# Forgetting attention in a two-layer decoder trunk: the running sums of log f enter the scores by an addition on VectorE instead of by matmuls

## The chip, the cores and the metric

The kernel runs on one core of one Trainium2 chip. The metric is the device time of one execution in microseconds. Before the change the median of three executions is 919.61 us (918.66 to 920.67).

## What is computed

A residual trunk of two layers works on 256 rows of width 2048. In each layer one normalised input is multiplied by one wide weight matrix, and the product feeds four groups of four heads: forgetting attention ("fox"), differential attention, block attention ("moba") and gated linear attention ("gla"). Their outputs are gated, joined and multiplied by an output matrix. The change touches only the fox group, of which this is the core:

```python
cum = jnp.cumsum(log_f.astype(jnp.float32), axis=-1)
logits = jnp.einsum("bhqd,bhkd->bhqk", q_i, k) * scale
logits = logits + c_i[..., :, None] - cum[:, :, None, :]
logits = jnp.where(k_pos[None, :] <= q_pos[:, None], logits, -jnp.inf)
p = jax.nn.softmax(logits, axis=-1)
```

Here `log_f` is the log-sigmoid of one number per row and head. The part that depends on the query alone falls out of the softmax, so the kernel adds only a row that runs over the keys, one row for each head.

## The kernel before

**The steps.** Each weight matrix is cut into blocks of up to 512 columns, and each block into steps of two or four tiles of 128 rows. For one step, SyncE issues the load of `raw` (L1106), ScalarE rounds it to `hi` (L426), VectorE subtracts to get `lo` (L429), and TensorE does 12 matmuls, or 24 for narrow blocks: the input's high part by `hi`, its low part by `hi`, its high part by `lo` (L1192 to L1196). `hi` and `lo` have four buffers each, so these two engines can prepare at most three steps beyond the one that TensorE is on. `raw` has four buffers as well. Blocks 0, 1 and 2 of a layer (gla's gate, gla's q and k, and a block that holds the four `fox_f` columns) run interleaved; block 2 accumulates in a `side` tile.

**The small work.** Everything else is written as generators in a list `tasks`. After each step's matmuls, `tick` (L257) goes through the list in order and lets each task emit instructions up to its next `yield`. It stops when the estimated cost put on VectorE or ScalarE passes what TensorE's work has allowed (L261, L1202). So the order of each engine's instructions is fixed when the program is built; an engine then executes its own list strictly in that order and waits for others by semaphores. A small product that is emitted after step n stands between step n and step n+1 in TensorE's list. Helpers `matmul` (L276) and the cost wrapper (L178) record most instructions, which is why the profile shows them under these two lines.

**The forgetting bias.** When block 2 is finished, `gla_gate` (L569) copies `fox_f` to `fx` and starts `fox_forget` (L812). This adds the bias, computes the log-sigmoid through three small ScalarE activations on `fe` (Abs, Exp, Ln; L529), forms `f` on VectorE and scales it. Then it rounds `f` to `fh` with a rest `fl`, and ScalarE multiplies two constant 128x128 triangles (`since`, part of the tile `ct`) by every column of both, 8 activations of 128x128 for each part and layer. The two results stay in two `four` tiles. Later `softmax_part` (L703) lets TensorE sum them over the partitions: a matmul with a tile of ones, `ones_r`, puts the row into all partitions of the score tile, and the head's product of q and k is accumulated on top. There are two such matmuls of 512 columns for each half of the keys, so six in a layer. VectorE adds the causal mask `neg4`, takes the maximum, and ScalarE does the exponentials.

**The gated linear attention beside it.** The task `gla` (L591) runs at the same time. It goes through ScalarE and VectorE to fill the tile `eight`, and issues groups of seven products `side<-tq,eight` (L661 to L664), which stand in TensorE's list between steps.

Of the kernel before, what the change touches and what calls it, by code (L numbers as in the profile page):

```python
# [13 lines left out]
F32 = mybir.dt.float32  # L14
F32R = mybir.dt.float32r
BF16 = mybir.dt.bfloat16
U8 = mybir.dt.uint8
AF = mybir.ActivationFunctionType
# [3 lines left out]
P = 128  # L22
# [185 lines left out]
def hybrid_trunk(  # L208
# [39 lines left out]
    def take_side():  # L248
        return (yield from side.take([P, 1024]))
# [24 lines left out]
    def matmul(out, lhsT, rhs, start, stop, tiles=1):  # L274
        left["pe"] += int(np.prod(rhs.shape[1:])) * (4 if lhsT.dtype == F32 else 1) / 2400.0 / tiles
        t_.matmul(out, lhsT, rhs, start=start, stop=stop)  # L276
# [70 lines left out]
    dng = cp.tile([P, DEPTH], F32, name="dng")  # L347
    gng = cp.tile([P, DEPTH], F32, name="gng")
    wa = cp.tile([17, DEPTH, 256], F32, name="wa")
    ones_r = cp.tile([P, P], F32R, name="ones_r")  # L350
    neg_b = cp.tile([P, P], BF16, name="neg_b")
    neg4 = neg_b[:, None, :].to_broadcast([P, H, P])
    halfpow = cp.tile([P, 8], F32, name="halfpow")
# [21 lines left out]
    def constants():  # L375

        yield from until(("h", 0, 3))
        nc.scalar.dma_start(wa[0:16], gla_wa2.rearrange("l r e -> r l e"))
        nc.scalar.dma_start(wa[16:17].rearrange("p l e -> p (l e)"), gla_ba.rearrange("(o l) e -> o (l e)", o=1))
        yield  # L380
        c, n = CAT["masks"]
        mb = s4.get([P, n], BF16)
        nc.scalar.dma_start(mb, const_b[:, c:c + n])
        yield
        c, n = CAT["neg"]
        nc.scalar.dma_start(neg_b, const_b[:, c:c + n])
        nc.scalar.dma_start(gng, gla_norm_gt)
        nc.scalar.dma_start(fb.rearrange("p l h -> p (l h)"), bcast_rows(fox_fb, 0, DEPTH * H))
        yield
        lamt = s2.get([P, DEPTH, 4, 64])  # L390
        nc.scalar.dma_start(lamt.rearrange("p l a d -> p (l a d)"), bcast_rows(diff_lam, 0, DEPTH * 256))
        nc.scalar.dma_start(dng, diff_norm_gt)
        yield
        v_.tensor_copy(masks.rearrange("p l t -> p (l t)"), mb)
        v_.tensor_scalar(ones_r, ident, 0.0, 1.0, op0=OP.mult, op1=OP.add)
        s4.put(mb)
        ready.add("constants")
        yield
        lp = s2.get([P, DEPTH, 2, 64])
        for l in range(DEPTH):  # L400
            v_.tensor_mul(lp[:, l], lamt[:, l, 0:4:2], lamt[:, l, 1:4:2])
            v_.tensor_reduce(ls2[:, l], lp[:, l], axis=AX.X, op=OP.add)
        s2.put(lp, lamt)
        yield
        a_.activation(ls2, ls2, AF.Exp)
        yield
        for l in range(DEPTH):
            li = 0.8 - 0.6 * math.exp(-0.3 * l)
            v_.scalar_tensor_tensor(lam[:, l:l + 1], ls2[:, l, 0:1], li, ls2[:, l, 1:2], op0=OP.add, op1=OP.subtract)
            v_.tensor_scalar(dng[:, l:l + 1], dng[:, l:l + 1], 1.0 - li, None, op0=OP.mult)  # L410
# [14 lines left out]
    def hi_of(hi, src, scale=1.0):  # L425
        a_.activation(hi, src, AF.Copy, scale=scale)  # L426

    def lo_of(lo, src, hi):
        v_.tensor_sub(lo, src, hi.bitcast(F32))  # L429
# [139 lines left out]
    def gla_gate(l, ps):  # L569
        r, sg = env["r", l], env["gla_sg", l]  # L570
        vn = s4.get([P, 2, GW])
        fx = sm.tile([P, 2, H], F32, name="fx", bufs=2)
        for m in range(2):
            a_.activation(fx[:, m], ps[m][:, 180:184], AF.Copy, scale=r[:, m:m + 1])
            a_.activation(sg[:, m, 332:], ps[m][:, :180], AF.Silu, scale=r[:, m:m + 1])
            a_.activation(vn[:, m, :164], ps[m][:, 184:], AF.Copy, scale=r[:, m:m + 1])
        env["fox_v", l] = vn
        env["forget", l] = Forget()
        tasks.append(fox_forget(l, fx, env["forget", l]))

    def gla_v(l, ps):

# [120 lines left out]
    def softmax_part(m, qT, kT, rows, scale, su, forget=None):  # L703

        ps = yield from take_side()
        S = ps.rearrange("p (j h s) -> p j h s", j=2, h=H)
        for kt in range(m + 1):
            dst = S[:, kt]
            if forget is not None:
                forget(dst, kt)  # L710
            for h in range(H):
                matmul(dst[:, h], qT[rows, m * H + h], kT[1][rows, kt * H + h],
                       forget is None, forget is None or h == H - 1)
        yield
        v_.tensor_add(S[:, m], S[:, m], neg4)
        mx = sm.tile([P, H], F32, name="mx")
        if m == 0:
            v_.tensor_reduce(mx, S[:, 0], axis=AX.X, op=OP.max)
        else:
            v_.tensor_reduce(mx, S.rearrange("p j h s -> p h j s"), axis=AX.XY, op=OP.max)  # L720
        nb = sm.tile([P, H], F32, name="nb")
        v_.tensor_scalar(nb, mx, -scale, None, op0=OP.mult)
        yield
        if m == 0:
            p = yield from s2.take([P, H, P])
        else:
            p = yield from s4.take([P, H, 2, P])
        for h in range(H):
            a_.activation(p[:, h], S[:, 0, h] if m == 0 else S[:, :, h], AF.Exp, bias=nb[:, h:h + 1], scale=scale,
                          accum_out=su[:, m, h:h + 1])  # L730
            if h == 1:
                yield
        side.put(ps)
        return p
# [7 lines left out]
    def attend(l, gi, name, qT, kT, forget=None):  # L742

        su = sm.tile([P, 2, H], F32, name="su")
        rs = sm.tile([P, 2, H], F32, name="rs")
        boxes = []
        for m, pool in enumerate((s2, s4)):
            p = yield from softmax_part(m, qT, kT, slice(0, P), HD ** -0.5, su, forget)
            if m:
                s4.put(qT, kT[0])  # L750
                if forget is not None:
                    forget.release()
            v_.reciprocal(rs[:, m], su[:, m])
            for h in range(H):
                a_.activation(p[:, h], p[:, h], AF.Copy, scale=rs[:, m, h:h + 1])
            yield
            boxes.append(spawn(turned_p(p, m, partial(pool.put, p))))
        yield from until((name + "_v", l))
        yield from until((name + "_g", l))
        t0, p0 = yield from joined(boxes[0])  # L760
        t1, p1 = yield from joined(boxes[1])
        yield
        vn, (sgt, sg) = env[name + "_v", l], env[name + "_g", l]
        ops = yield from take_side()
        o = ops.rearrange("p (m h t) -> p m h t", m=2, h=H)
        for h in range(H):
            v0, v1 = (vn[:, j, h * P:(h + 1) * P] for j in range(2))
            matmul(o[:, 0, h], v0, p0[:, h], True, True)
            matmul(o[:, 1, h], v0, p1[:, 2 * h], True, False)
            matmul(o[:, 1, h], v1, p1[:, 2 * h + 1], False, True)  # L770
        s2.put(t0)
        s4.put(t1, vn)
        yield
        mixed = yield from s4.take([P, 2 * H, P])
        v_.tensor_mul(in_squares(mixed), ops.rearrange("p (x i r) -> p x i r", i=4, r=32), sg)
        side.put(ops)
        s4.put(sgt)
        yield
        yield from split_group(l, gi, mixed)
# [9 lines left out]
            matmul(o[:, 1, h], pt[2][:, h], vn[:, 1, h * P:(h + 1) * P], False, True)  # L789
        return o, ops  # L790

    class Forget:

        def __init__(self):
            self.fg = []

        def __call__(self, dst, kt):
            matmul(dst, ones_r, self.fg[0][:, kt], True, False)  # L800
            matmul(dst, ones_r, self.fg[1][:, kt], False, False)

        def release(self):
            s4.put(*self.fg)

    def fox_v(l, ps):
        r, vn = env["r", l], env["fox_v", l]
        for m in range(2):
            a_.activation(vn[:, m, 164:], ps[m], AF.Copy, scale=r[:, m:m + 1])
        ready.add(("fox_v", l))  # L810

    def fox_forget(l, fx, forget):  # L812
        yield
        v_.tensor_add(fx, fx, fb[:, l, None, :].to_broadcast([P, 2, H]))
        e = sm.tile([P, 2, H], F32, name="fe", bufs=2)
        f = sm.tile([P, 2, H], F32, name="f", bufs=2)
        yield from log_sigmoid(f, fx, e)
        v_.tensor_scalar(f, f, math.sqrt(HD), None, op0=OP.mult)
        yield
        fh = sm.tile([P, 2, H], F32R, name="fh", bufs=2)  # L820
        fl = sm.tile([P, 2, H], F32R, name="fl", bufs=2)
        hi_of(fh, f)
        lo_of(fl, f, fh)
        yield
        for part in (fh, fl):
            z = yield from s4.take([P, 2, H, P], F32R)
            pf = part.bitcast(F32)
            for m in range(2):
                for h in range(H):
                    a_.activation(z[:, m, h], since[m], AF.Copy, scale=pf[:, m, h:h + 1])  # L830
            forget.fg.append(z)
            yield
        ready.add(("forget", l))

    def fox(l):
# [455 lines left out]
```

## Time and profile before

| what | value |
|---|---|
| median of three executions | 919.61 us |
| the profiled execution's own time | 920.54 us |
| its span, first to last instruction | 918.8 us |
| TensorE matmul busy | 901.3 us, 98% of the span |
| VectorE busy | 571.5 us, 62% |
| ScalarE busy | 524.6 us, 57% |
| mean granted TensorE clock | 0.995 |
| HBM traffic | 223 GB/s over the span |

Lines of the profile give an engine, an operation, `out<-in` by the program's names with buffer numbers left out, the shape and a count. In a timeline the first two numbers are the start and the length in us of a merged run of equal instructions, so neighbouring rows overlap a little; what stands in brackets is the idle time before the first of them and what ended it. PE is TensorE, DVE is VectorE, ACT is ScalarE, POOL is GpSimd, SP is SyncE. A matmul on 32-bit operands that are not rounded (type `f32` in the program) appears as two records.

### The profile page before, as it was taken

What the parts mean: (1) busy time and instruction counts of PE and PEld (TensorE: products, weight loads), DVE (VectorE), ACT (ScalarE), POOL (GpSimd) and SP (SyncE); (2) the same over time, 40 slices, a digit from 0 to 9 for tenths busy, and PEclk for the clock granted to TensorE, in tenths of its full rate; (3) what the DMA queues carried; (4) which work ended last, traced back from release to release, by engine and by line L of the source; (5) the groups of instructions that cost most, each with busy time, mean ns of one, the idle gap of its engine ahead of it and who ended that gap; (6) DMA issues with size and microseconds to landing.
All of it is one profiled execution on the core that took longest, in us unless ns stands there. A gap on an engine that the chain in (4) does not pass through costs nothing.

```text
span 918.8 us, 12421 instructions
## 1 busy us (share of the span) xinstructions
PE 901.3 (98%) x4490; PEld 766.8 (83%) x4490; DVE 571.5 (62%) x831; ACT 524.6 (57%) x819; POOL 38.6 (4%) x55
## 2 busy tenths in 40 slices
PE   8999999999999999999999999999999999999996
PEld 6988789888888888888899887988888888878886
DVE  6765887566558556555655568856655674565662
ACT  6588654664455556535565784566444654754441
POOL 0000000000000010000000000010000000110000
PEclk9999999999999999999999999999999999999998
DMA  8767656587656947757776466667877687587652
GB/s 264 255 206 263 234 182 240 167 301 263 233 183 205 319 156 236 276 200 259 235 231 212 145 235 194 192 212 213 290 231 228 172 264 274 159 307 254 193 164 92
DMA packets 77455, 205.34 MB, mean 223 GB/s; under 512 B 9265, under 2 KB 29137, under 8 KB 77394
## 3 DMA queue, kind: packets, MB, share of 16 engines
q1 hardware_dynamic: 70496, 183.44, 60.7%
q0 software_dynamic: 5408, 19.40, 6.1%
q10 hardware_dynamic: 1490, 1.71, 0.6%
q8 instruction: 35, 0.57, 0.2%
q14 instruction: 26, 0.21, 0.1%
HBM read 184.07 MB, written 20.45 MB: 223 GB/s over the span
## 4 chain that ended last, share of the span: by engine, by line
PE 86%; DMA 4%; ACT 3%; DVE 2%; issue 2%; SPq 1%; DVEq 0%; POOLq 0%; POOL 0%; ACTq 0%
PE mm L276 77%; PE side L276 9%; DMA four<-far 3%; DMA far<-four 1%; ACT hi L178 1%; ACT four L178 1%; DVE lo L178 1%; SPq L310 1%; DMA raw<-in_weights 1%; ACT L178 0%; DVE four L178 0%; DVE tq L178 0%; DVE eight L178 0%; ACT two L178 0%; DVE two L178 0%
## 5 line engine op out<-in xcount | busy, mean ns | idle before, releaser
L178 DVE TENSOR_TENSOR lo<-raw,hi 128x1024 fp32r<-128x1024 f32 (+1 forms) x316 | 368.4, 1170 | 305.4 <-ACT hi L178 288.5
L178 ACT ACTIVATE hi<-raw 128x1024 fp32r<-128x1024 f32 (+1 forms) x316 | 319.1, 1017 | 301.6 <-PE mm L276 244.1
L276 PE MATMUL mm<-hi,hTp 128*128 128x512 f32 (+1 forms) x1920 | 461.3, 382 | 2.6 <-ACT hi L178 2.6
L276 PEld LDWEIGHTS mm<-hi,hTp 128*128 128x128 f32 x1920 | 352.3, 188 | 68.1 <-ACT hi L178 3.9
L276 PE MATMUL mm<-lo,hTp 128*128 128x512 f32 (+1 forms) x960 | 248.3, 380 | 0.0
L276 PEld LDWEIGHTS mm<-lo,hTp 128*128 128x128 f32 x960 | 177.8, 188 | 32.7
L276 PE MATMUL mm<-hi,mTh 128*128 128x512 f32 (+1 forms) x256 | 64.6, 377 | 0.0
L276 PE MATMUL mm<-hi,mTl 128*128 128x512 f32 (+1 forms) x256 | 64.4, 376 | 0.0
L276 PE MATMUL mm<-lo,mTh 128*128 128x512 f32 (+1 forms) x256 | 64.4, 376 | 0.0
L276 PEld LDWEIGHTS mm<-lo,mTh 128*128 128x128 f32 x256 | 46.2, 188 | 8.8
L276 PEld LDWEIGHTS mm<-hi,mTl 128*128 128x128 f32 x256 | 46.2, 188 | 8.7
L276 PEld LDWEIGHTS mm<-hi,mTh 128*128 128x128 f32 x256 | 46.1, 188 | 8.7
L312 POOL DMA_DIRECT2D four<-far x32 | 17.2, 538 | 617.2 <-DMA far<-four 266.3
L276 PE MATMUL side<-four,four 128*128 128x128 f32 (+1 forms) x320 | 37.3, 277 | 1.9 <-DMA four<-far 1.9
L276 PEld LDWEIGHTS side<-four,four 128*128 128x128 f32 (+1 forms) x320 | 34.1, 190 | 4.6 <-DMA four<-far 2.5
L178 DVE STREAM_TRANSPOSE four<-four 128x1024 f32<-128x1024 f32 x24 | 29.5, 1230 | 0.0
L178 ACT ACT_TABLE_LOAD x22 | 28.2, 1283 | 0.3
L178 ACT ACTIVATE four<-mm,rstd 128x512 f32<-128x512 f32 (+1 forms) x40 | 24.4, 661 | 0.1
L276 PE MATMUL side<-hi,hTp 128*128 128x348 f32 x128 | 22.9, 321 | 0.0
L178 ACT ACTIVATE four<-side 32x64 f32<-32x64 f32 (+2 forms) x28 | 8.8, 342 | 24.3 <-PE side L276 24.3
L276 PEld LDWEIGHTS side<-hi,hTp 128*128 128x128 f32 x128 | 20.8, 188 | 1.3 <-issue 0.7
L178 ACT ACTIVATE four<-side,nb 128x256 f32<-128x256 f32 (+1 forms) x48 | 20.4, 437 | 1.5 <-DVE nb L178 1.2
(135 smaller groups left out, 500.1 us busy)
## 6 DMA issues: line engine op xcount, KB each, us to landing
raw<-in_weights SPq DMA_DIRECT2D x272, 512.0 KB, 4.3
far<-four SPq DMA_DIRECT2D x128, 128.0 KB, 4.2
four<-far POOLq DMA_DIRECT2D x32, 512.0 KB, 6.4
raw<-in_weights SPq DMA_DIRECT2D x47, 348.0 KB, 3.4
xs<-in_x SPq DMA_DIRECT2D x4, 512.0 KB, 5.1
four<-in_xt SPq DMA_DIRECT2D x3, 512.0 KB, 5.6
far<-two SPq DMA_DIRECT2D x24, 64.0 KB, 3.6
two<-far POOLq DMA_DIRECT2D x6, 256.0 KB, 5.2
```

The source lines that it names most:

```text
L178: return f(*args, **kw)
L276: t_.matmul(out, lhsT, rhs, start=start, stop=stop)
L310: nc.sync.dma_start(d[:, :, i].rearrange("j c f -> c j f"), t[32 * i:32 * i + 32].rearrange("c (j f) -> c j f", j=4))
L312: g_.dma_start(t, d.rearrange("j c i f -> (j c) (i f)"))
```

## The change

The two rounded parts, the 32 scaled triangles, the tile `ones_r` and the matmuls with it are gone. In their place `fox_forget` does two small fp32 products with `f` itself (128 rows by 4 heads) as the stationary side and a constant triangle as the moving side. They give the sums as 4 rows of 2x128 in a `side` tile. VectorE copies them to `cum`, SyncE writes `cum` to DRAM, and GpSimd issues a transfer that reads it back into all 128 partitions of one `four` tile. In `softmax_part` the q-k products of fox now start and stop by themselves, and VectorE adds the tile to the scores.

```diff
-            dst = S[:, kt]
-            if forget is not None:
-                forget(dst, kt)
             for h in range(H):
-                matmul(dst[:, h], qT[rows, m * H + h], kT[1][rows, kt * H + h],
-                       forget is None, forget is None or h == H - 1)
+                matmul(S[:, kt, h], qT[rows, m * H + h], kT[1][rows, kt * H + h], True, True)
         yield
         v_.tensor_add(S[:, m], S[:, m], neg4)
+        if forget is not None:
+            v_.tensor_add(S[:, :m + 1], S[:, :m + 1], forget[:, :m + 1])
...
-        def __call__(self, dst, kt):
-            matmul(dst, ones_r, self.fg[0][:, kt], True, False)
-            matmul(dst, ones_r, self.fg[1][:, kt], False, False)
...
         yield from log_sigmoid(f, fx, e)
         v_.tensor_scalar(f, f, math.sqrt(HD), None, op0=OP.mult)
         yield
-        fh = sm.tile([P, 2, H], F32R, name="fh", bufs=2)
-        fl = sm.tile([P, 2, H], F32R, name="fl", bufs=2)
-        hi_of(fh, f)
-        lo_of(fl, f, fh)
-        yield
-        for part in (fh, fl):
-            z = yield from s4.take([P, 2, H, P], F32R)
-            pf = part.bitcast(F32)
-            for m in range(2):
-                for h in range(H):
-                    a_.activation(z[:, m, h], since[m], AF.Copy, scale=pf[:, m, h:h + 1])
-            forget.fg.append(z)
-            yield
+        ps = yield from take_side()
+        for m in range(2):
+            matmul(ps[:H, m * P:(m + 1) * P], f[:, m], since[m], True, True)
+        yield
+        c = sm.tile([H, 2, P], F32, name="cum", bufs=2)
+        v_.tensor_copy(c, ps[:H, :SEQ].rearrange("h (m s) -> h m s", m=2))
+        side.put(ps)
+        yield
+        d = yield from far.take([1, 2, H, P])
+        nc.sync.dma_start(d[0].rearrange("m h s -> h m s"), c)
+        yield
+        z = yield from s4.take([P, 2, H, P])
+        g_.dma_start(z.rearrange("p m h s -> p (m h s)"), d.rearrange("o m h s -> o (m h s)").to_broadcast([P, 2 * H * P]))
+        far.put(d)
+        for _ in range(LANDS):
+            yield
+        env["forget", l] = z
         ready.add(("forget", l))
```

The order of the engines' instructions shifts with it. The first place is TensorE's list in layer 0, from the end of block 2 on. `side_250` and `side_249` are block 2's accumulator, and each pair of `mm<-hi` and `mm<-lo` rows is one step. Before:

```order
L276 MATMUL side_250<-hi,hTp 128x348 x8
L276 MATMUL side_250<-lo,hTp 128x348 x4
L276 MATMUL mm<-hi,hTp 128x512 x8
L276 MATMUL mm<-lo,hTp 128x512 x4
L276 MATMUL mm<-hi,hTp 128x512 x8
L276 MATMUL mm<-lo,hTp 128x512 x4
L276 MATMUL mm<-hi,hTp 128x512 x8
L276 MATMUL mm<-lo,hTp 128x512 x4
L276 MATMUL mm<-hi,hTp 128x512 x8
L276 MATMUL mm<-lo,hTp 128x512 x4
L276 MATMUL mm<-hi,hTp 128x512 x8
```

The same place in the changed kernel:

```order
L276 MATMUL side_249<-hi,hTp 128x348 x8
L276 MATMUL side_249<-lo,hTp 128x348 x4
L276 MATMUL mm<-hi,hTp 128x512 x8
L276 MATMUL mm<-lo,hTp 128x512 x4
L276 MATMUL mm<-hi,hTp 128x512 x8
L276 MATMUL mm<-lo,hTp 128x512 x4
L276 MATMUL mm<-hi,hTp 128x512 x8
L276 MATMUL mm<-lo,hTp 128x512 x4
L276 MATMUL mm<-hi,hTp 128x512 x8
L276 MATMUL mm<-lo,hTp 128x512 x4
L276 MATMUL side_791<-ct,f 4x128 x2
L276 MATMUL mm<-hi,hTp 128x512 x8
```

The two new products stand behind the fourth 512-column step after block 2, ahead of the fifth. Layer 1 has them at the same place.

The second place is VectorE's list around `f`, again in layer 0, where the tile `eight` belongs to gated linear attention. Before:

```order
L178 TENSOR_TENSOR lo<-raw,hi 128x1024
L178 SCALAR_TENSOR_TENSOR f<-fx,fe 128x8
L178 TENSOR_SCALAR f<-f 128x8
L178 TENSOR_TENSOR lo<-raw,hi 128x1024
L178 TENSOR_TENSOR fl<-f,fh 128x8
L178 TENSOR_TENSOR lo<-raw,hi 128x1024 x4
L178 TENSOR_TENSOR eight_900<-two_738 128x2x64 x2
```

The same place in the changed kernel:

```order
L178 TENSOR_TENSOR lo<-raw,hi 128x1024
L178 SCALAR_TENSOR_TENSOR f<-fx,fe 128x8
L178 TENSOR_SCALAR f<-f 128x8
L178 TENSOR_TENSOR lo<-raw,hi 128x1024 x2
L178 COPY cum<-side_791 4x256
L178 TENSOR_TENSOR lo<-raw,hi 128x1024 x3
L178 TENSOR_TENSOR eight_885<-two_736 128x2x64 x2
```

What leads up to `f` is the same; the copy `cum` takes the place of `fl`, one subtraction later.

The third place is TensorE's list at gated linear attention's first products of layer 0 (`side<-tq,eight`, and `side<-eight` behind them). Before:

```order
L276 MATMUL mm<-hi,hTp 128x512 x8
L276 MATMUL mm<-lo,hTp 128x512 x4
L276 MATMUL mm<-hi,hTp 128x512 x8
L276 MATMUL mm<-lo,hTp 128x512 x4
L276 MATMUL side_1116<-tq,eight_900 128x128 x7
L276 MATMUL mm<-hi,hTp 128x512 x8
L276 MATMUL mm<-lo,hTp 128x512 x4
L276 MATMUL side_1150<-tq,eight_900 128x128 x7
```

The same steps in the changed kernel:

```order
L276 MATMUL side_1061<-tq,eight_885 128x128 x7
L276 MATMUL mm<-hi,hTp 128x512 x8
L276 MATMUL mm<-lo,hTp 128x512 x4
L276 MATMUL side_1095<-tq,eight_885 128x128 x7
L276 MATMUL mm<-hi,hTp 128x512 x8
L276 MATMUL mm<-lo,hTp 128x512 x4
L276 MATMUL side_1133<-eight_885 128x128 x2
```

The first group of seven has moved ahead by two steps, and the second with it; layer 1 has the same move. From the q-k products of fox on, TensorE's list is as before, without the `ones_r` rows.

More of the change, by code (lines that the diff above doesn't have):

```diff
@@ L349, in hybrid_trunk @@
     wa = cp.tile([17, DEPTH, 256], F32, name="wa")
-    ones_r = cp.tile([P, P], F32R, name="ones_r")
     neg_b = cp.tile([P, P], BF16, name="neg_b")
@@ L394, in constants @@
         v_.tensor_copy(masks.rearrange("p l t -> p (l t)"), mb)
-        v_.tensor_scalar(ones_r, ident, 0.0, 1.0, op0=OP.mult, op1=OP.add)
         s4.put(mb)
@@ L577, in gla_gate @@
         env["fox_v", l] = vn
-        env["forget", l] = Forget()
-        tasks.append(fox_forget(l, fx, env["forget", l]))
+        tasks.append(fox_forget(l, fx))
     def gla_v(l, ps):
@@ L751, in attend @@
                 if forget is not None:
-                    forget.release()
+                    s4.put(forget)
             v_.reciprocal(rs[:, m], su[:, m])
@@ L790, in rows_product @@
         return o, ops
-    class Forget:
-        def __init__(self):
-            self.fg = []
-        def __call__(self, dst, kt):
-            matmul(dst, ones_r, self.fg[0][:, kt], True, False)
-            matmul(dst, ones_r, self.fg[1][:, kt], False, False)
-        def release(self):
-            s4.put(*self.fg)
     def fox_v(l, ps):
@@ L810, in fox_v, with fox_forget @@
         ready.add(("fox_v", l))
-    def fox_forget(l, fx, forget):
+    def fox_forget(l, fx):
         yield
```

## The prediction

> **What bounds the kernel now.** I read the page first, then the waits of TensorE, then the timelines around the place where the new products stand. The page says how busy the engines are, the waits say for what TensorE sat idle (in all, times, longest):
>
> ```profile
> PE 901.3 (98%) x4490; PEld 766.8 (83%) x4490; DVE 571.5 (62%) x831; ACT 524.6 (57%) x819; POOL 38.6 (4%) x55
> PE side L276 <- DVE eight L178: 3.0, 2, 1.7
> PE mm L276 <- ACT hi L178: 2.6, 2, 2.1
> PE side L276 <- DMA four<-far: 1.9, 3, 1.0
> ```
>
> TensorE works nearly without a gap, so in the middle of the program every microsecond that its list gains or loses goes to the end of the run, and work on VectorE or ScalarE counts only where TensorE ends up waiting for it. Of the idle time, 3.0 us belong to gated linear attention (`eight`), once in each layer.
>
> **TensorE work that goes and comes.** In layer 0 the removed matmuls stand here:
>
> ```profile
> 158.66 0.64 PE L276 MATMUL side<-four,ones_r 128*128 128x512 f32 x2
> 159.13 1.05 PE L276 MATMUL side<-four,four 128*128 128x128 f32 x8
> 159.94 2.09 PE L276 MATMUL mm<-hi,hTp 128*128 128x512 f32 x8
> ...
> 170.95 0.64 PE L276 MATMUL side<-four,ones_r 128*128 128x512 f32 x2
> 171.43 1.05 PE L276 MATMUL side<-four,four 128*128 128x128 f32 x8
> 172.24 0.71 PE L276 MATMUL side<-four,ones_r 128*128 128x512 f32 x2
> 172.78 1.05 PE L276 MATMUL side<-four,four 128*128 128x128 f32 x8
> ```
>
> From start to start the three pairs take 0.47, 0.48 and 0.54 us, 1.49 us a layer, 2.98 us in both. What comes is two fp32 products a layer. By the q-k rows, eight records of 128 columns take 0.81 us (159.13 to 159.94), so two products of two records take 0.41. I take 0.45 a layer, 0.9 in both, for a 4-column stationary side is not in the trace; the ends are zero and 2.1 (double the q-k price, with their ends in the open). The balance of the work is -2.1 us.
>
> **The wait that comes.** The products stand behind the fourth 512-column step after block 2 and need the scaled `f`. The stretch in layer 1, TensorE first, then what leads up to `f` on ScalarE and VectorE:
>
> ```profile
> 511.78 2.00 PE L276 MATMUL mm<-hi,hTp 128*128 128x512 f32 x8
> ...
> 519.97 1.98 PE L276 MATMUL mm<-hi,hTp 128*128 128x512 f32 x8
> 522.69 1.98 PE L276 MATMUL mm<-hi,hTp 128*128 128x512 f32 x8
> 526.12 2.11 PE L276 MATMUL mm<-hi,hTp 128*128 128x512 f32 x8 [0.55 <-ACT hi L178]
> ...
> 521.87 0.21 ACT L178 ACTIVATE fe<-fx 128x8 f32<-128x8 f32 x1 [2.69 <-DVE fx L178]
> 522.10 1.28 ACT L178 ACT_TABLE_LOAD   x1
> ...
> 523.62 1.28 ACT L178 ACT_TABLE_LOAD   x1
> 524.91 0.21 ACT L178 ACTIVATE fe<-fe 128x8 f32<-128x8 f32 x1
> 525.03 2.00 ACT L178 ACTIVATE hi<-raw 128x1024 fp32r<-128x1024 f32 x2
> ...
> 526.10 1.23 DVE L178 TENSOR_TENSOR lo<-raw,hi 128x1024 fp32r<-128x1024 f32 x1 [4.32 <-ACT hi L178]
> 527.44 0.17 DVE L178 TENSOR_SCALAR f<-f 128x8 f32<-128x8 f32 x1
> ```
>
> The first step behind block 2 starts at 511.78 and a step takes 2.72 us (519.97 to 522.69), so the fourth is over at 522.69. `f` is ready at 527.44 + 0.17 = 527.61: two table loads stand ahead of it, and VectorE takes a `lo` first whose `hi` comes after the third `fe`. Nothing in this chain is touched by the change, and nothing in it waits for TensorE's fifth step. With about 0.15 us from VectorE's end to TensorE's start (first `eight` at 560.33, 0.28 us long, products at 560.76), TensorE stands still from 522.69 to 527.75, 5.1 us. Before, nobody on TensorE asked for `f`; it was only an input of ScalarE's triangles. Layer 0 is the same with a shorter chain:
>
> ```profile
> 71.92 1.98 PE L276 MATMUL mm<-hi,hTp 128*128 128x512 f32 x8
> 74.64 1.98 PE L276 MATMUL mm<-hi,hTp 128*128 128x512 f32 x8
> 78.11 0.17 DVE L178 TENSOR_SCALAR f<-f 128x8 f32<-128x8 f32 x1
> ```
>
> There the fourth step ends at 74.64 and `f` is ready at 78.28: 3.8 us. Behind the products in TensorE's list is the main work itself, so nothing hides these 8.9 us. ScalarE and VectorE can use the time for three steps at most, since `hi` and `lo` have four buffers.
>
> **Waits that go.** The 0.55 us ahead of 526.12 lies within the new wait. The two waits for `eight` are these:
>
> ```profile
> 111.43 1.80 PE L276 MATMUL side<-tq,eight 128*128 128x128 f32 x14 [1.28 <-DVE eight L178]
> 557.99 1.07 PE L276 MATMUL mm<-lo,hTp 128*128 128x512 f32 x4
> 560.76 1.80 PE L276 MATMUL side<-tq,eight 128*128 128x128 f32 x14 [1.70 <-DVE eight L178]
> ```
>
> The products now stand two steps (5.44 us) earlier, but TensorE comes to every step later by the wait and the two products, 4.25 us in layer 0 and 5.0 in layer 1. So `eight` is wanted about 2.5 and 2.1 us earlier than it came (5.44 - 4.25 + 1.28; 5.44 - 5.0 + 1.70). On the other side the list ahead of it loses the two groups of triangles,
>
> ```profile
> 528.71 2.44 ACT L178 ACTIVATE four<-ct,fh 128x128 fp32r<-128x128 f32 x8
> 531.05 1.04 ACT L178 ACTIVATE hi<-raw 128x1024 fp32r<-128x1024 f32 x1
> 532.00 2.44 ACT L178 ACTIVATE four<-ct,fl 128x128 fp32r<-128x128 f32 x8
> 534.34 1.04 ACT L178 ACTIVATE hi<-raw 128x1024 fp32r<-128x1024 f32 x1
> ```
>
> 2.34 us each from start to start, and two `hi` of 0.95 us that now stand behind: 6.6 us where ScalarE is the bound, less where it waits for TensorE to free a buffer. Even half of it is enough. I count both waits as gone, -3.0 us, and keep +1.5 for the case that half stays.
>
> **The clock.** A long gap has a price of its own in this kernel. Three stretches of the length in which the clock changes, and what follows the third; each row gives its length, the busy time of PE, PEld, DVE, ACT and POOL, the granted clock, and the load of DMA:
>
> ```profile
> 5.61:9.03 3.42, 1.36 (x9) 1.33 (x9) 2.09 (x5) 2.17 (x4) 0.00 (x0) 1.00 1.02 385
> 9.03:12.44 3.41, 3.41 (x14) 3.41 (x13) 2.34 (x3) 2.91 (x4) 0.00 (x0) 0.50 0.89 257
> 558.57:561.98 3.41, 1.71 (x14) 1.31 (x13) 3.37 (x11) 0.68 (x1) 0.00 (x0) 1.00 0.53 187
> 561.98:565.39 3.41, 3.41 (x21) 2.89 (x19) 3.34 (x7) 1.53 (x4) 0.00 (x0) 1.00 0.68 247
> ```
>
> TensorE was idle for 2.05 us of the first stretch, and the clock was 0.50 in the whole of the next. In the third it was idle for 1.70 us, and the clock stayed at 1.00. So I take it that 3.41 us with more than about 1.9 us of idle cost half the clock in the next 3.41 us. Where the gaps fall against these stretches is not known, so I average over the place u in its stretch at which a gap begins, and a microsecond at half clock costs 0.5 us. Layer 0, 3.8 us: for u below 1.5 (44%) the next stretch is slow, and 3.05 - u of it is work, 1.15 us lost on average; above that the stretch after it is slow, 1.65 lost; mean 1.4. Layer 1, 5.1 us: u below 0.25 (7%) loses 0.8; 0.25 to 1.5 (37%) makes both following stretches slow, 0.45 + 1.7; up to 1.8 (8%) loses 1.7; above it (48%) 1.3; mean 1.6. Together 3.0 us, between 1.5 and 4.0.
>
> The Trainium skill, TensorE: Matmul & The Clock Gate, Part 1, says that the clock falls to half after at least one idle window of about 3.4 us, on a grid that runs freely. Read as a wholly idle window it would rarely catch the first gap and the second about every other time, some 1 us in place of the 3.0; the first stretch above, with 1.36 us of work in it, speaks for the stricter reading, and the length of the windows agrees.
>
> **What is beside the path.** VectorE gains two additions a layer, sized by its mask and reduction rows, and the copy; SyncE and GpSimd gain one issue each:
>
> ```profile
> L178 DVE TENSOR_TENSOR side<-side,neg_b 128x512 f32<-128x512 f32 x12 | 8.3, 691 | 5.5 <-PE side L276 5.5
> L178 DVE TENSOR_TENSOR four<-side,four 128x1024 f32<-128x1024 f32 x4 | 4.9, 1221 | 2.1 <-PE side L276 2.1
> L178 DVE COPY at<-side 16x256 f32<-16x256 f32 x2 | 0.8, 405 | 0.0
> four<-far POOLq DMA_DIRECT2D x32, 512.0 KB, 6.4
> ```
>
> The additions (0.69 and 1.22 us) delay fox's maximum; behind them on VectorE is a `lo` that TensorE wants up to three steps (8.2 us) later, which is their cover. The transfer back is issued some three steps behind the products, near 87 us in layer 0, and wanted after 159.94; if its 6.4 us became 60 it would still land in time. Behind the write of `cum` on SyncE stand weight loads, which run up to four steps ahead of their use. Zero for all of it; the price without cover would be at most 1.2 us a layer, from a transposed tile that lands late.
>
> **The sum.** -2.98 + 0.9 + 3.8 + 5.1 - 0.55 - 2.98 + 3.0 = +6.3 us. On the profiled execution's 920.54 that gives 926.8; it lies 0.9 us above the median of 919.61, so I put the same difference on the median: 925.9 us.
>
> **The rivals.**
> - *The clock stays.* The gaps come, but a gap with work on either side of a stretch does not lower the clock. Then the sum is +3.3 us, 922.9. For it: the two gaps of 1.28 and 1.70 us did nothing to the clock, though they are shorter. Against: the stretch from 5.61. By the rule of the Trainium skill named above in its literal reading it would be 923.9, between the two. 20%.
> - *Faster: the products find `f` ready.* If TensorE reached the products after `f`, only the saved 2.1 us and the waits of 3.5 us would count: 914.0. The point is a fourth step that ends after 78.3 and 527.6; it would have to come 3.6 and 4.9 us later than before, or the chain with its table loads as much earlier. Nothing ahead of it in either list has changed. 5%.
> - *More waits.* `eight` still late by half, and fox's longer softmax turned into a late tile at its output product, where layer 1 had 0.31 us of the 1.9 us for `four<-far`: 1.5 + 0.5 more, 927.9. For it: the products stand earlier. 9%.
> - *No change.* The gaps are half as long (4.5 us less), because the log-sigmoid gets through sooner than in this trace, and the clock costs 1.5 us less: +0.3, 919.9. 5%.
>
> **How the numbers follow.** My forecast keeps 61%. About 0.2% (1.8 us) is what a measurement of this kernel can tell from no change. Faster has the second rival's 5%; within 0.2% the last one's 5% and a little of the first, 6%; slower the rest, 89%. The range goes from the first rival with a slightly shorter gap, 922.2, to the forecast with the clock's upper end and `eight` half late, 919.6 + 6.3 + 1.0 + 1.5 = 928.4.
>
> **What would show it.** In the changed kernel's waits TensorE should wait for VectorE's `f` twice, 3 to 5.5 us each; the wait for `eight` should be gone; no wait for the added tile or for `cum`; the granted clock at 0.5 for one to three stretches of 3.41 us, all right behind the two gaps. I am wrong if there is no wait for `f`, if the clock stays at 1 behind 5 us of idle, or if ScalarE falls behind again.

## The result and the profile after

The changed kernel takes 929.83 us (median of four executions, 928.63 to 930.52) against 919.61 us (918.66 to 920.67). The ratio is 1.0107, interval 1.0092 to 1.0122: slower by 10.2 us. The forecast was 925.9 us with a range up to 928.4, so the direction came as forecast and the loss is larger than the range. The profiled execution took 930.40 us, 9.9 us more than that of before.

TensorE's waits after, in the form shown before (in all, times, longest):

```profile
PE side L276 <- DVE f L178: 8.5, 2, 4.9
PE side L276 <- DMA four<-far: 3.0, 3, 2.2
PE mm L276 <- ACT hi L178: 2.1, 1, 2.1
```

The wait for `f` is there twice, with the forecast's length (8.5 us, forecast 8.9), and the wait for `eight` is gone. The wait for `four<-far` has grown from 1.9 to 3.0 us. The timeline of TensorE at the two new places and at the last output product of layer 1:

```profile
73.79 1.07 PE L276 MATMUL mm<-lo,hTp 128*128 128x512 f32 x4
78.49 1.01 PE L276 MATMUL side<-ct,f 128*4 128x128 f32 x4 [3.63 <-DVE f L178]
79.43 3.78 PE L276 MATMUL mm<-hi,hTp 128*128 128x512 f32 x8
83.01 1.71 PE L276 MATMUL mm<-lo,hTp 128*128 128x512 f32 x4
84.56 2.00 PE L276 MATMUL mm<-hi,hTp 128*128 128x512 f32 x8
...
531.99 1.01 PE L276 MATMUL side<-ct,f 128*4 128x128 f32 x4 [4.91 <-DVE f L178]
532.93 3.03 PE L276 MATMUL mm<-hi,hTp 128*128 128x512 f32 x8
...
835.40 1.22 PE L276 MATMUL side<-four,four 128*128 128x128 f32 x4 [2.24 <-DMA four<-far]
```

Eight matmuls that took 1.98 us before take 3.78 us behind the first wait and 3.03 behind the second, without a gap between them. The granted clock in its own stretches shows why (length, busy time of PE, PEld, DVE, ACT, POOL, granted clock, DMA):

```profile
74.12:77.53 3.41, 0.74 (x4) 0.28 (x2) 0.70 (x1) 3.38 (x5) 0.00 (x0) 1.00 0.57 192
77.53:80.94 3.41, 2.45 (x8) 1.60 (x9) 3.38 (x6) 1.16 (x2) 0.70 (x1) 0.50 0.52 165
80.94:84.36 3.42, 3.42 (x10) 2.65 (x9) 0.02 (x1) 1.06 (x1) 0.00 (x0) 0.50 0.88 279
84.36:87.77 3.41, 3.41 (x17) 2.79 (x16) 1.30 (x2) 1.17 (x2) 0.00 (x0) 1.00 0.94 355
528.09:531.50 3.41, 0.00 (x0) 0.00 (x0) 1.17 (x2) 3.40 (x5) 0.53 (x1) 1.00 0.36 123
531.50:534.92 3.42, 2.93 (x9) 1.99 (x10) 2.92 (x6) 0.69 (x1) 0.00 (x0) 0.50 0.78 291
...
831.87:835.29 3.42, 1.28 (x7) 0.94 (x5) 2.99 (x3) 1.40 (x2) 0.00 (x0) 1.00 1.00 340
835.29:838.70 3.41, 3.30 (x15) 3.31 (x16) 0.92 (x1) 1.06 (x1) 0.00 (x0) 0.50 1.03 412
```

Four stretches of half clock in mid-run, where the forecast named one to three, all right behind the two gaps: two behind the first wait, one behind the second, and one behind a wait of 2.24 us for a transposed tile that has no `f` in it. In work lost they cost half of 84.36 - 78.49, of 534.92 - 531.99 and of 838.70 - 835.40: 2.9 + 1.5 + 1.65 = 6.0 us.

VectorE's additions and the copy stand beside the path with the forecast's lengths; nobody on TensorE waits for them:

```profile
80.56 0.41 DVE L178 COPY cum<-side 4x256 f32<-4x256 f32 x1
...
167.81 0.70 DVE L178 TENSOR_TENSOR side<-side,four 128x512 f32<-128x512 f32 x1
...
179.39 1.23 DVE L178 TENSOR_TENSOR side<-side,four 128x1024 f32<-128x1024 f32 x1
```

### The profile page after: what moved, and what is told of

Same layout as the page of the kernel before. It is cut to its first block, busy times and chain, and to the rows that moved or that the text cites. A ratio compares the mean times of both kernels' runs of the same rounds, so it can differ in the third digit from the quotient of the medians.

```text
span 928.5 us, 12387 instructions
## 1 busy us (share of the span) xinstructions
PE 905.0 (97%) x4486; PEld 769.3 (83%) x4486; DVE 576.6 (62%) x834; ACT 516.6 (56%) x785; POOL 39.7 (4%) x57
## 3 DMA queue, kind: packets, MB, share of 16 engines
q10 hardware_dynamic: 1490, 1.71, 0.6%
## 4 chain that ended last, share of the span: by engine, by line
PE 87%; DMA 5%; ACT 2%; DVE 2%; issue 2%; SPq 1%; POOLq 0%; POOL 0%; DVEq 0%; ACTq 0%
PE mm L276 78%; PE side L276 9%; DMA four<-far 3%; DMA raw<-in_weights 2%; DMA far<-four 1%; ACT hi L178 1%; DVE lo L178 1%; ACT L178 1%; ACT two L178 0%; DVE four L178 0%; SPq L310 0%; DVE two L178 0%; ACT four L178 0%; ACT fe L178 0%; DVE xs L178 0%
```

## The experiments

Theory A: the change costs what TensorE waits for `f` at two places, and the half clock behind it. Theory B, the rival: the loss over the forecast comes from the transfer back and VectorE's additions, which delay tiles later on. Fifteen runs followed, in four groups; each group ran on one chip beside the kernel before, whose medians there are 920.5, 920.7, 920.4 and 921.0 us. What follows is sorted by question, so some paragraphs hold runs of two groups.

### One part at a time

**Products two steps later** (`late2`).

```diff
+        for _ in range(2):
+            yield
         ps = yield from take_side()
         for m in range(2):
             matmul(ps[:H, m * P:(m + 1) * P], f[:, m], since[m], True, True)
```

> Changed kernel with the two products placed two steps later (behind the sixth step after block 2 instead of the fourth). Theory A (the loss is TensorE's wait for f at two places, and the half clock behind it): no wait for f, no half clock in the middle of the program; 919.6 - 2.1 = 917.5 us if gated linear attention's wait of 3.0 us is back in full, 914.5 us if it stays away. Theory B (the loss over the forecast comes from the transfer back and VectorE's additions, which are still there): only the gaps go, about 921 us, with a longer wait for a transposed tile at the last product.

921.03 us, ratio 0.9994 (0.9970 to 1.0018). TensorE no longer waits for `f`, and there is no half clock behind either place:

```profile
79.18 1.07 PE L276 MATMUL mm<-lo,hTp 128*128 128x512 f32 x4
80.17 0.60 PE L276 MATMUL side<-ct,f 128*4 128x128 f32 x4
80.70 2.11 PE L276 MATMUL mm<-hi,hTp 128*128 128x512 f32 x8
```

The step of two yields takes the whole loss back, as theory A has it. The time is theory B's 921 us, though, and not theory A's 917.5 or 914.5: 1.6 us of waiting for `eight` return in its profile (3.0 before), and 2.3 us for `four<-far`. That profiled execution took 917.99 us, 3 us less than the median, so what the others lost is not seen. The rows also give the products' price at full clock, 0.53 us.

**The gap filled** (`warm16`).

```diff
         ps = yield from take_side()
+        for _ in range(16):
+            t_.matmul(ps[:, 512:640], ident, ident, start=True, stop=True)
         for m in range(2):
```

> Changed kernel with 16 products of a constant by itself put ahead of the two products in each layer; they need no f, take about 3.5 us (32 records of 0.11 us) and leave out nothing of the computation. TensorE still comes on to the next step only after f. Theory A: the wait for f shrinks to 0.1 us in layer 0 and 1.4 us in layer 1, the step behind it starts at the same time as in the changed kernel, the clock stays at 1.0 behind both places; 929.8 - 4.5 = 925.3 us, and 923 us if the longer wait at the last product goes as well. Theory B, or a loss that has nothing to do with the clock: 929.8 us or more.

926.24 us, ratio 1.0063 (1.0041 to 1.0084): near theory A's 925.3 and below theory B's 929.8, with a spread from 923.3 to 928.5. In its profile the filling covers the first gap, and the matmuls behind it run at full speed, 2.11 us in place of 3.78:

```profile
73.04 3.73 PE L803 MATMUL side<-ct 128*128 128x128 f32 x32
76.73 0.60 PE L276 MATMUL side<-ct,f 128*4 128x128 f32 x4
77.27 2.11 PE L276 MATMUL mm<-hi,hTp 128*128 128x512 f32 x8
```

The same profile has a wait for a transposed tile that is longer than the one at 835.40 in the changed kernel, and no half clock behind it. The idle time falls into two stretches, and each of them holds over 2 us of work:

```profile
829.83 0.71 PE L276 MATMUL side<-four,four 128*128 128x128 f32 x4 [2.55 <-DMA four<-far]
```

```profile
825.20:828.62 3.42, 2.08 (x11) 1.58 (x9) 3.03 (x3) 1.53 (x2) 0.00 (x0) 1.00 0.92 301
828.62:832.03 3.41, 2.20 (x19) 2.20 (x20) 0.68 (x1) 1.06 (x1) 0.00 (x0) 1.00 1.00 394
832.03:835.44 3.41, 3.41 (x19) 2.86 (x18) 1.77 (x2) 1.00 (x2) 0.00 (x0) 1.00 0.99 386
```

**The products alone, in the kernel before** (`prod_only`).

```diff
         v_.tensor_scalar(f, f, math.sqrt(HD), None, op0=OP.mult)
         yield
+        ps = yield from take_side()
+        for m in range(2):
+            t_.matmul(ps[:H, m * P:(m + 1) * P], f[:, m], since[m], start=True, stop=True)
+        side.put(ps)
         fh = sm.tile([P, 2, H], F32R, name="fh", bufs=2)
```

> Kernel before with the two products added at the place where the changed kernel has them; their result is not used, all the rest is as before (triangles, matmuls with ones, no transfer, no addition). Theory A: wait for f of 3.6 and 4.9 us, half clock behind it; 919.6 + 0.9 + 8.5 - 0.55 - 3.0 + 4.5 = 930.0 us (927 to 931). Theory B: about 920.5 us.

930.93 us, ratio 1.0126 (1.0102 to 1.0150). Theory A's 930.0 is met: two products whose result nobody reads cost the kernel before as much as the whole change. That the two losses are so alike is in part chance: the matmuls with ones still run here, while waits for `four<-far` are 1.4 us shorter than before (0.5 in place of 1.9). The wait for `f` is the same, and the clock stays at half for two stretches behind both places. The wait, and the second place:

```profile
PE side L822 <- DVE f L178: 8.5, 2, 4.9
```

```profile
531.07:534.48 3.41, 1.34 (x5) 0.78 (x6) 2.96 (x6) 2.78 (x6) 0.53 (x1) 0.50 0.33 89
534.48:537.90 3.42, 3.42 (x9) 2.65 (x9) 0.96 (x1) 2.04 (x8) 0.00 (x0) 0.50 0.99 367
537.90:541.30 3.40, 3.40 (x16) 2.80 (x16) 1.23 (x1) 3.40 (x10) 0.00 (x0) 1.00 0.46 174
```

**Without transfer and additions** (`no_use`), the bias left out.

```diff
-        d = yield from far.take([1, 2, H, P])
-        nc.sync.dma_start(d[0].rearrange("m h s -> h m s"), c)
...
-        env["forget", l] = z
+        env["forget", l] = None
```

> Changed kernel without the transfer (neither the write of the four rows nor the read back) and without VectorE's additions of the tile, so the forgetting bias is left out of the scores; the products and the copy stay. Theory A: as the changed kernel, 929.8 us within 1.5. Theory B: about 926 us, the forecast's value, and the wait at the last product back at 1.0 us.

925.81 us, ratio 1.0061 (1.0042 to 1.0080): the value of theory B, and not theory A's. But its profile gives a reason without the transfer. TensorE's list is the same as in the changed kernel. The waits for `f` are as long as ever, 3.63 and 4.91 us, and each has only one stretch of half clock behind it; here is the first:

```profile
74.52:77.93 3.41, 0.94 (x6) 0.66 (x7) 2.56 (x5) 2.67 (x3) 0.70 (x1) 1.00 0.28 84
77.93:81.35 3.42, 3.42 (x10) 2.65 (x9) 1.53 (x3) 0.35 (x1) 0.00 (x0) 0.50 0.97 367
81.35:84.76 3.41, 3.41 (x17) 2.78 (x16) 1.23 (x1) 1.46 (x2) 0.00 (x0) 1.00 0.94 330
```

So the next group put this kernel beside the changed one.

### The same pair on one chip, and late products with and without the rest

**The changed kernel again** (`after_again`), and **without transfer and additions again** (`no_use_again`), both without a new edit.

> The changed kernel itself, beside the next three. Theory A: again a wait for f of 3.6 and 4.9 us with half clock behind it, and a wait at the output products near 380 and 830 us that differs from run to run (0 to 2.5 us in the six profiles so far); if that wait stays under 1.9 us there is no third half clock. 926 to 930 us. Theory B: the wait near 830 us is again over 2 us and the half clock stands behind it.

> The changed kernel without the transfer and VectorE's additions once more (the forgetting bias is left out), on the same chip as the changed kernel. Theory A: the same time as the changed kernel within 1.5 us. Theory B: 4 us less.

928.98 us (ratio 1.0071, 1.0044 to 1.0099) and 929.08 us (1.0081, 1.0057 to 1.0105). Theory B falls for the changed kernel: without its transfer and additions it is as slow, as far as intervals of 5 us can tell. In both profiles each gap now has two stretches of half clock behind it, and no third gap has any. The first two of TensorE's waits of `after_again`; those for `four<-far` are two in place of three, and the longest is 1.4 us in place of 2.2:

```profile
PE side L276 <- DVE f L178: 8.5, 2, 4.9
PE side L276 <- DMA four<-far: 2.6, 2, 1.4
```

The two profiles of the kernel without the transfer, 923.65 and 930.11 us, also differ before anything of the change has run. The first eight matmuls of the main work, first in `no_use`, then in `no_use_again`:

```profile
7.76 1.55 PE L276 MATMUL mm<-hi,hTp 128*128 128x348 f32 x8 [2.12 <-ACT hi L178]
```

```profile
7.96 2.69 PE L276 MATMUL mm<-hi,hTp 128*128 128x348 f32 x8 [2.31 <-ACT hi L178]
```

The slow start costs `no_use_again` 2.6 us by 14 us into the program. In the profiles before and after the change the first slow stretch begins at 9.03 and 9.26 us, so the start is no part of their difference.

**Late products without transfer and additions** (`late2_no_use`: the edits of `late2` and `no_use` together, the bias left out), and both once more on another chip (`late2_again`, `late2_no_use2`).

> Products two steps later, and without the transfer and VectorE's additions (the forgetting bias is left out). No gap and no half clock cover anything here, so what the transfer and the additions cost shows against the kernel with late products alone, 921.0 us beside 920.5 for the kernel before. Theory A: 921 us within 1.5. Theory B: 917 us.

> Products two steps later, transfer and additions in place, on one chip with the kernel without them. If the transfer and the additions cost nothing where no gap covers them: as the next kernel within 1 us, some 918 to 921 us. If they cost something there (by the two earlier values 921.0 and 917.8): 2 to 3 us more than the next kernel, with the longer wait in the places where TensorE waits for four<-far.

> The same without the transfer and VectorE's additions (the forgetting bias is left out). Costs nothing: as the kernel above within 1 us. Costs something: 2 to 3 us less.

917.76 us (0.9965, 0.9946 to 0.9983) for the first: near theory B's 917 and outside theory A's 921 within 1.5. On one chip, 919.62 us with transfer and additions (0.9984, 0.9965 to 1.0003) and 917.90 without (0.9971, 0.9955 to 0.9987): 1.7 us, between the two expected values. The comparisons point to 1 to 3 us, but the intervals overlap and no profile shows a wait of TensorE for the tile. Whether the transfer and the additions cost 1 to 3 us where no gap covers them stays open.

### A better version, and the loss without the varying waits

**Gated linear attention's first products one step later as well** (`late2_gla1`, and again as `late2_gla1_again`), on top of `late2`.

```diff
+            if pair == 0:
+                for _ in range(1):
+                    yield
             for m in range(2):
                 pcs = yield from take_side()
```

> Products two steps later, and gated linear attention's first seven products of each layer one step later as well. Theory A: no wait for f and none for its tile eight (1.0 and 0.6 us with late products alone); TensorE's list is 2.1 us shorter than before and 3.0 us of waits are gone: 920.5 - 5 = 915.5 us. Theory B: no gain over 920.5 us.

> Both delays (products two steps, gated linear attention's first products one step). Theory A: 1.5 us below the products' delay alone, the price of the two waits for eight in its profile, less where waits for four<-far grow; 917 to 919 us, below the kernel before.

918.62 us (0.9965, 0.9947 to 0.9983) and 917.28 us (0.9945, 0.9925 to 0.9965): faster than the kernel before, by 2.0 and 3.1 us on the medians (3.2 and 5.1 by the ratios). The first misses its 915.5, the second lies in its range. The wait for `eight` is gone, but what is late next is again a transposed tile. The first line of TensorE's waits of `late2_gla1_again`:

```profile
PE side L276 <- DMA four<-far: 4.8, 3, 1.9
```

**Readers of transposed tiles one step later** (`gla1_lands5`), on top of `late2_gla1`. `LANDS` is the number of yields between the issue of a transfer back and the tasks that read its tile.

```diff
-LANDS = 4
+LANDS = 5
```

> Both delays, and every task that reads a transposed tile goes on one step later (LANDS 5 in place of 4). In the profile with both delays TensorE waited 3.8 us for four<-far at three places, once long enough for half clock. If those waits come from products that stand too early behind a transfer, 1 to 3 us go: 915 to 917 us. If the longer chain makes TensorE run dry at the end of a layer instead, 920 us or more.

913.66 us, from 912.7 to 913.9 in six executions; ratio 0.9915, 0.9897 to 0.9934. This is the fastest of all, its spread is the smallest, and it lies below the 915 to 917 expected. TensorE waits for no transfer back any more; all its waits are these:

```profile
PE mm L276 <- ACT hi L178: 2.6, 2, 2.1
PE side L367 <- DVE halfpow L361: 1.2, 1, 1.2
```

**The same later readers in the kernel before, the changed kernel and the filled one** (`before_lands5`, `after_lands5`, `warm16_lands5`; the edit of one line as above). What was open was how much of the excess is clock and how much the varying waits for transposed tiles.

> Kernel before with every reader of a transposed tile one step later. It takes TensorE's waits for four<-far (1.9 us in its profile) out; 918 to 919 us against 920.4. It is the base for the next two kernels, whose difference to it holds neither those waits nor their spread.

> Changed kernel with the same later readers. If the excess over the forecast is half clock that stays on for a second stretch of 3.41 us: two waits for f of 8.5 us in all, 10 to 14 us of half clock, no wait for four<-far; 7.5 to 9 us over the kernel before with later readers. If the excess is the waits for four<-far: 5 to 6.5 us over it, the forecast's +6.3.

> Changed kernel with later readers and the 16 filling products in the two gaps. The place and length of the gaps for everything but the filling stay; the clock stays at 1.0. It is below the changed kernel with later readers by the price of the half clock: 4.5 to 5.5 us if each gap costs one to two stretches, 3.0 us by the forecast.

The kernel before falls to 917.04 us (ratio 0.9954, 0.9940 to 0.9969), below the 918 to 919 expected: 4.0 us less than the median beside it, though the waits in the profile before were 1.9. So part of the last version's gain is not the change's. The changed kernel takes 923.66 us (1.0031, 1.0018 to 1.0044) and the filled one 920.01 us (0.9989, 0.9979 to 0.9999). Without the waits for `four<-far` the change costs 6.6 us by the medians and 7.1 by the ratios: between the 5 to 6.5 us expected if the excess is those waits and the 7.5 to 9 us expected if it is the clock. The filling gives back 3.65 us, between the forecast's 3.0 and the 4.5 to 5.5 expected. TensorE's waits of `after_lands5`, where no transposed tile is left:

```profile
PE side L276 <- DVE f L178: 8.5, 2, 4.9
PE mm L276 <- ACT hi L178: 2.2, 1, 2.2
PE side L367 <- DVE halfpow L361: 1.2, 1, 1.2
```

The best version against the kernel before with later readers is 913.66 against 917.04, 3.4 us, on two chips. This is not what the change itself is worth. The best version also has gated linear attention's first products one step later, and the kernel before with later readers still waits for `eight`:

```profile
PE side L276 <- DVE eight L178: 3.4, 2, 1.7
```

No run has the kernel before with both delays, so the change's own share is not shown. From the table below an estimate is 1.9 us, the work that TensorE no longer has (2.98 less 1.1).

## Why the prediction was right and wrong

**Right.** The sum's main terms held. In the table, measured values are those of the two profiled executions (920.54 and 930.40 us):

| term | forecast | measured | from |
|---|---|---|---|
| matmuls with ones go | -2.98 | -2.98 | not run any more |
| new products, at full clock | +0.9 | +1.1 | 0.53 a layer in `late2` |
| wait for `f` | +8.9 | +8.5 | 3.63 + 4.91 |
| wait for `hi` inside it | -0.55 | -0.55 | gone |
| waits for `eight` | -2.98 | -2.98 | gone |
| half clock in mid-run | +3.0 | +6.0 | four stretches |
| waits for `four<-far` | 0 | +1.1 | 1.9 to 3.0 |
| sum | +6.3 | +10.2 | the executions differ by 9.9 |

That the wait is the cause is shown by `prod_only` and `late2`: the products alone bring a loss as large, and moving them two steps takes it away. That half clock behind the gaps is a part of it is shown by the filling, which takes 3.65 us off with later readers. For the transfer and the additions `no_use_again` shows no cost in the changed kernel; with late products it stays open.

**Wrong, first: the step on the clock.** The prediction averaged over where a gap falls and let half clock end after the stretch, unless that next stretch was itself idle for more than 1.9 us. It did not ask how a stretch counts that is already slow. The term of 3.0 us measured 4.4 behind the two gaps, and the excess lies in layer 0: 2.9 against 1.4, where layer 1 has 1.5 against 1.6. The profiles answer the question: after 2.45 us of TensorE work at half clock (77.53), and 2.10 and 1.83 us in `after_again`, the next stretch was slow again, although TensorE was idle in them for only 0.96 to 1.6 us. After 2.93 us (531.50) and 3.42 us (77.93 in `no_use`) it was not. The 1.34 us at 531.07 in `prod_only`, with 2.07 us of idle, are what the prediction's rule covers. The two stretches of `after_again`, and one at the start of the changed kernel, which half clock followed as well:

```profile
78.34:81.76 3.42, 2.10 (x7) 1.34 (x8) 3.38 (x6) 1.53 (x2) 0.70 (x1) 0.50 0.41 157
532.32:535.73 3.41, 1.83 (x6) 1.17 (x7) 3.38 (x5) 1.79 (x2) 0.53 (x1) 0.50 0.48 137
```

```profile
5.85:9.26 3.41, 1.55 (x10) 1.55 (x11) 2.29 (x5) 2.38 (x5) 0.00 (x0) 1.00 1.05 410
9.26:12.67 3.41, 3.41 (x13) 3.41 (x13) 2.75 (x4) 3.39 (x4) 0.00 (x0) 0.50 0.80 212
```

At full clock the boundary thus lies between 1.55 us of work and the 1.71 us that the prediction read from before; at half clock it lies between 2.45 and 2.93. Halving the second pair (1.2 and 1.5) does not quite make one rule of the two, for 1.55 us at full clock did not keep the clock. A gap that took 0.96 us of the slow stretch was paid twice, one that took 0.49 us of it (531.50) once. The rival in which the clock stays is dead. The stretches from 74.12 and 831.87 were enough for half clock with 0.74 and 1.28 us of work in them. The Trainium skill, TensorE: Matmul & The Clock Gate, Part 1, asks for an idle window; read as a wholly idle one, it does not fit these two.

**Wrong, second: the step "zero for all of it".** The waits for `four<-far` were taken as unchanged because no term touched them. In the thirteen profiles of kernels with LANDS 4 they are 0.5 to 4.8 us in all, and in the changed kernel one of 2.24 us at 835.40 drew half clock, 1.65 us more. With later readers, where they are gone, the change costs 6.6 us, close to the forecast's 6.3, so the two explanations share the excess. That it comes so close is in part luck. The profile of `after_lands5` still has three slow stretches in mid-run, worth 4.5 us in place of 3.0 by the same count; against that, the wait for `f` is 0.4 us shorter than forecast, and its base loses 3.4 us of waits for `eight` in place of 2.98. By the table's terms, the profiled pair is 3.9 us over the forecast: 1.4 for half clock behind the two gaps (4.4 against 3.0), 1.65 for the third place, 1.1 for the longer waits, and -0.2 for the products and the wait for `f` together. On medians the shares cannot be told to better than 2 us, since the loss itself was 10.2 us on the first chip and 8.3 on the second. Why these waits lengthen in the changed kernel is not settled; `no_use_again` has them at 2.7 us without the added transfer.

**The other rivals.** The faster one needed a fourth step that ends after `f`; `late2` shows that the point was right, though not the price, since `eight` and `four<-far` wait instead. "More waits" did not come as described: `eight` was not late, and fox's output product in layer 1, named there with 0.31 us, waits 0.24 us after the change; the tile that came late belongs to another product, at 835.40. That nothing changes is ruled out by the interval, 1.0092 to 1.0122.

## What to carry to other kernels

When a small product is moved onto the busiest engine, look up in the trace when its operand is ready against where the product will stand in that engine's list: here it stood 3.6 and 4.9 us too early for it. Two yields, which place the product behind its operand, took back the whole loss. A gap on TensorE can be paid a second time in clock, and where it falls decides: the gaps of 3.63 and 4.91 us were paid so in all six profiles that have them unfilled, one of 2.24 us was, one of 2.55 us that lay across two stretches was not. Before a difference of some tenths of a per cent is judged, take out waits that vary by themselves: one step more for the readers of transposed tiles took TensorE's waits for them out of all four profiles that have it, and made the kernel faster.

## What was not expected of the hardware

- Half clock lasts: a stretch of 3.41 us at half clock with up to 2.45 us of matmuls in it was followed by another, with 2.93 us it was not.
- The grid of the stretches lies anywhere against the program. Within a profile, slow stretches begin whole multiples of 3.413 us apart; counted back in such steps, the grid's first edge lies from 0.24 us (`gla1_lands5`) to 3.29 us (`after_lands5`) behind the first instruction in the seventeen profiles. Where the same gap falls on the grid decides, as far as these rows show, between one slow stretch behind it and two. The first slow stretch begins at 77.93 us in `no_use`, with one behind each gap, and at 78.89 us in `no_use_again`, the same kernel, with two.
- The speed at the program's start varies as well: the first eight matmuls of the main work took 1.55 us in one profile and 2.69 us in another of the same kernel.
